# Two modulation chunks in another stage, and another order and other operands for two gates, in a two-layer decoder trunk

## The chip, the core and the metric

The kernel runs on one core of a Trainium2 chip. The core has five engines with instruction queues of their own: TensorE (PE, matrix products; its weight loads are listed as PEld), VectorE (DVE), ScalarE (ACT), GpSimd (POOL) and SyncE (SP, which here issues nearly all DMA transfers). They meet through semaphores. The metric is the device time of one execution in microseconds; lower is better. Times of repeated runs are compared by their median; one further execution is recorded by the hardware profiler.

## What is computed

The reference is a trunk of two layers on 256 tokens with 1,024 features, all in float32. A vector c sets shift, scale and gate (the modulation) of each of the four sub-layers. Cut to what matters here:

```python
for i in range(2):
    mod = silu(c) @ w_ada[i] + b_ada[i]          # 6 x 1024 values for each layer
    sh1, sc1, g1, sh2, sc2, g2 = split(mod, 6)
    h = rmsnorm(x) * (1 + sc1) + sh1
    y = dilated_mixture(h) if i == 0 else gla_mixer(h)
    x = x + g1 * y
    h = rmsnorm(x) * (1 + sc2) + sh2
    x = x + g2 * conv_ffn(h)
return rmsnorm(x)
```

The mixer of layer 0 is a mixture of three dilated window attentions with 16 heads. The mixer of layer 1 is a gated linear attention (GLA) with 4 heads in chunks of 64 tokens. For each chunk of a head it forms `A = causal(q_t @ k_t.T)`, `o = A @ v + q_t @ state`, and the mixer ends with `(rmsnorm(o) * silu(r)) @ w_out`, where r, the gate, is a product of h with 1,024 more columns. The channel mixer is `silu(a) * b` of two halves of a short convolution over `h @ w_up`, times w_down, with 2 x 2,816 columns.

## The kernel before

Features lie on the 128 partitions and the 256 tokens along the free dimension, so h is eight tiles of 128 x 256, one for each "k tile" of 128 features. To come near float32 with the fast float32r products each operand is split into a high and a low part, and each product is three matmuls (`mm3`, lines 199 to 201): high x high, low x high (the low part of h), and high x low (the low part of the weights). A weight tile is loaded by one DMA into a ring of four raw buffers (tile `raw`); ScalarE casts it into its high part (`whi`, line 172), and VectorE subtracts that from the raw data for the low part (`wlo`, line 178), each in two halves and into rings of three buffers (`split`).

The modulation is not a matrix product on TensorE. Its weights come in 48 chunks, 24 for each layer, each 1,024 KB, holding two columns of 128 outputs. A chunk is worked by `ada_dot` (line 140): for each half, VectorE multiplies 128 x 1,024 weights by silu(c), broadcast over the partitions, and sums them; then a small ScalarE operation (line 148 or 150) adds the bias. Eight chunks are worked at the start, where h is first built. The other 40 stand in the list `rest` and are taken in order, at places written out by hand: `next_half` takes half a chunk (512 KB) into one of three spare buffers of the attention stage, and `next_ada` takes a whole one into a buffer of the ring that the weights use.

The stages in order, on the profile's time axis: the start and the first products (to about 60 us); the attention by pairs of heads u = 0 to 7 (to about 287), where for u >= 2 each pair brings three query-key weight tiles (`wqk`, g = 0, 1, 2) and two value weight tiles (`wv`), and next_half is called behind each g; the output projection of layer 0; its up-projection (to about 419) in 22 column tiles of 48 matmuls each (`pab`), followed on VectorE by the convolution (lines 769, 771), the product (777) and the split of the result (779); its down-projection (`pd`, to about 479); the GLA (to about 573); its output projection (`py`, to 596); the up- and down-projection of layer 1; the final norm and output.

In the GLA, `states(hd)` forms a head's queries and keys (`pqk`), scales them on VectorE by the decays (k_d, q_t, k_t: lines 927 to 929), transposes k_d, and forms the products k_t x q_t (bank `a`, line 941), which VectorE copies through the causal mask into a_t (line 944). Then the states of the chunks follow (`kv`, line 951, and st, line 958). `products(hd)` forms the head's output from a_t, v, the states and q_t (bank `o`, lines 974 and 977), and `normed_output` norms it. `gate(n)` loads a weight tile of the gate (`w_r_b`) and forms its 48 matmuls into bank `pr`.

The order on each engine is fixed before the run. A scheduler goes through the program with a model of the engines' times: among the instructions that it holds ready on an engine it takes the first in program order, and it also places the buffers. `behind(i, ...)` makes instructions wait in that order until the named ones are issued. The program sets the gates between the heads' work as fillers for TensorE.

One more thing is set by hand: `shift(pool, columns)` places a pad, which moves the addresses of the tiles that the pool places behind it. A pad of 8 columns is 32 bytes on each partition. In the up-projections the column tiles i = 4 and 12 take, for the k tiles 6 and 7, copies of h (tile `lv`, made by ScalarE at line 740) that lie elsewhere in the memory. By the addresses that the kernel's tiles are given, the weights lie at 32 modulo 128 bytes, h at 96, and these copies at 32: level with the weights.

The few lines that the change touches most:

```python
def next_ada():
    if rest:
        ada_chunk(*rest.pop(0))
...
s2 = states(2)
output(1, *s1)
s3 = states(3)
po2 = products(2, *s2)
gate(0)
...
```

Of the kernel before, what the change touches and what calls it, by code (L numbers as in the profile page):

```python
# [57 lines left out]
def trunk(ctx: ExitStack, tc: tile.TileContext, I, out):  # L58
# [294 lines left out]
    def parts(w, at, n=P):  # L353
        return w[0][:, at : at + n], w[1][:, at : at + n]
# [225 lines left out]
    for u in range(NPAIR):  # L580
        with tc.issue_after(last_load[0].ins):
            bias = load_bias(u)
        q = [q_pair[u % 2]]
        k = [[att.tile([P, T + 4], F32R, tag=f"k0{i}", name="k") for i in range(2)]]
        for z in k[0]:
            nc.gpsimd.memset(z[:, T:].bitcast(F32), 0.0)
        for g in (1, 2):
            q.append(att.tile([P, T], F32, tag=f"q{g}", name="q"))
            k.append(att.tile([P, T], F32, tag=f"k{g}", name="k"))
        v = [att.tile([P, NG * P], F32, tag=f"v{t}", name="v") for t in range(2)]  # L590
        if u == 0:
            b0 = [bank("pqk", tg) for tg in "ssspp"]
            pqk = [b[:, T * i : T * i + T] for b in b0[:3] for i in range(2)]
            pv = b0[3:]
            b1 = [bank("pqk", "t") for _ in range(3)]
            pqk1 = [b[:, T * i : T * i + T] for b in b1 for i in range(2)]
            for kt in range(KT):
                s, e = kt == 0, kt == KT - 1

                for a, b in ((0, 0), (1, 0), (0, 1)):  # L600
                    for i in range(2 * NG):
                        w = parts(w0[kt], P * i)
                        mm(pqk[i], w[a], h[kt][b], start=s and i % 2 == 0 and (a, b) == (0, 0), stop=e and i % 2 == 1 and b == 1)  # L603
                wv = parts(w0[kt], 6 * P, NG * P)
                for a, b in ((0, 0), (1, 0), (0, 1)):
                    for t in range(2):
                        mm(pv[t][:, : NG * P], h[kt][a][:, P * t : P * t + P], wv[b], start=s and (a, b) == (0, 0), stop=e and b == 1)
                for i in range(2 * NG):
                    mm3(pqk1[i], parts(w0[kt], 9 * P + P * i), h[kt], s and i % 2 == 0, e and i % 2 == 1)
        if u < 2:  # L610
            for g in range(NG):
                evacuate(q, k, g, (pqk, pqk1)[u][2 * g], (pqk, pqk1)[u][2 * g + 1])
        else:
            for g in range(NG):
                w = split(I["wqk"][u - 2, g], 2048)
                pqk = bank("pqk", "p")
                pq, pk = pqk[:, :T], pqk[:, T:]
                for kt in range(KT):
                    s, e = kt == 0, kt == KT - 1
                    mm3(pq[:, :T], parts(w, 2 * P * kt), h[kt], s, False)  # L620
                    mm3(pk[:, :T], parts(w, 2 * P * kt + P), h[kt], False, e)
                done = evacuate(q, k, g, pq, pk)
                if (u, g) == (2, 0):
                    first_loads.append(last_load[0])
                    for _ in range(2):
                        next_half(outputs[0])

                for _ in range((3, 3 if u == 2 else 1, 2)[g]):
                    next_half(outputs[u - 1] if g == 1 else done)
            if u == 2:  # L630
                with behind(last_load[0]):
                    nc.sync.dma_start(x_all, I["xT"])
        if u > 0:
            pv = [bank("pv", "p") for _ in range(2)]
            for half in range(2):
                with behind(*chain[7]):

                    w = split(I["wv"][u - 1, half], 1536, after=((first_values,) if u == half == 1 else (), ()))
                for k4 in range(4):
                    kt = 4 * half + k4  # L640
                    wv = parts(w, 384 * k4, 384)
                    for t in range(2):
                        ht = [y[:, P * t : P * t + P] for y in h[kt]]
                        last_pv[:] = [mm3(pv[t][:, :384], ht, wv, kt == 0, kt == KT - 1)]
        for n in range(2):
            copies = by_group(v[n], pv[n], n)
            if u == n == 0:
                first_values = copies
        outputs.append(attend(u, q, k, v, bias))
# [67 lines left out]
    def ffn(l, early):  # L717
# [10 lines left out]
        with tc.tile_pool(name=f"ffn{l}", bufs=2) as pool:  # L728
# [6 lines left out]
            for i in range(NFF):  # L735
                if i == 2:
                    with behind(*chain[7]):
                        for kt in level:
                            for s in range(2):
                                nc.scalar.copy(level[kt][s], h[kt][s])  # L740
                if i == 0:

                    pab, pab1 = bank("pab", "t"), bank("pab")
                    for kt in range(KT):
                        mm3(pab[:, :T], parts(w_early[0], P * kt), h[kt], kt == 0, kt == KT - 1)
                        for s in range(2):
                            mm3(pab1[:, T * s : T * s + T], parts(w_early[1], 2 * P * kt + P * s), h[kt],
                                kt == 0 and s == 0, kt == KT - 1 and s == 1)
                    with behind(*chain[5]):
                        pu = [whole(pool.tile([P, T], F32, tag="u", name="u")), pab[:, :T]]  # L750
                elif i == 1:
                    pu = [pab1[:, :T], pab1[:, T:]]
                else:
                    with behind(*(chain[5], chain[7])[min(i - 2, 1)]):
                        w = split(I["w_up"][l, i], 2048)
                    pab = bank("pab")
                    pu = [pab[:, :T], pab[:, T:]]
                    for kt in range(KT):
                        hk = level.get(kt, h[kt]) if i in (4, 12) else h[kt]
                        for s in range(2):  # L760
                            mm3(pu[s], parts(w, 2 * P * kt + P * s), hk, kt == 0 and s == 0, kt == KT - 1 and s == 1)
                ab = []
                for s in range(2):
                    f = i + NFF * s
                    cw = [col(C_CW + 132 * l + 44 * j + f) for j in range(3)]
                    r = pool.tile([P, T], F32, tag=f"r{s}", name="r")
                    u = pu[s]
                    nc.scalar.activation(r, u[:, :T], AF.Identity, scale=cw[2], bias=col(C_CB + 44 * l + f))  # L768
                    nc.vector.scalar_tensor_tensor(r[:, 1:T], u[:, 0 : T - 1], cw[1], r[:, 1:T],
                                                   op0=ALU.mult, op1=ALU.add)  # L770
                    nc.vector.scalar_tensor_tensor(r[:, 2:T], u[:, 0 : T - 2], cw[0], r[:, 2:T],  # L771
                                                   op0=ALU.mult, op1=ALU.add)
                    ab.append(r)
                sa = pool.tile([P, T], F32, tag="sa", name="sa")
                silu = nc.scalar.activation(sa, ab[0], AF.Silu)
                g32 = pool.tile([P, T], F32, tag="g32", name="g32")
                nc.vector.tensor_tensor(g32, sa, ab[1], op=ALU.mult)
                nc.scalar.copy(g_hi[i], g32)
                last_g = nc.vector.tensor_tensor(g_lo[i], g32, g_hi[i].bitcast(F32), op=ALU.subtract)
                if l == 0 and i % 5 == 4 and i < 20:  # L780
                    with behind(*chain[7]):
                        next_ada()
            exp_ln_after(silu)
# [37 lines left out]
    nc.vector.tensor_scalar(nbg, small[:, C_BG : C_BG + 4], -1.0, None, op0=ALU.mult)  # L821

    PARTS = ((0, 1), (1, NH_B - 1))
    keep = gt([P, (NH_B - 1) * T], "keep", tag="D1")
    nc.gpsimd.memset(keep, 1.0)
    nc.gpsimd.memset(keep.rearrange("p (n c) -> p n c", c=CH)[:, :, 0:1], 0.0)
# [76 lines left out]
        nc.vector.tensor_copy(v[t][:, 512:D], pv[t][1])  # L903

    o_n = []
    turned_keys = []

    def states(hd):
        if hd == 0:
# [28 lines left out]
        pa = bank("a", "s")  # L938
        for t in range(2):
            c = slice(P * t, P * t + P)  # L940
            mm(pa[:, c], k_t[:, c], q_t[:, c], start=True, stop=True)
        a_t = gt([P, 2, P], "a_t", bufs=2)
        nc.gpsimd.memset(a_t, 0.0)
        nc.vector.copy_predicated(a_t, causal.bitcast(U32), pa[:, :T].rearrange("p (a b) -> p a b", a=2))
# [52 lines left out]
    def gate(n):  # L997

        w = split(I["w_r_b"][n], 2048, **({} if n else dict(after=(turned_keys[:1], ()), low=turned_keys[1:])))
        pr = bank("pr", "p")  # L1000
        for kt in range(KT):
            for s in range(2):
                with behind(*((), last_o, norm_ops[:1], ())[n]):
                    mm3(pr[:, T * s : T * s + T], parts(w, 2 * P * kt + P * s), h[kt],
                        kt == 0 and s == 0, kt == KT - 1 and s == 1)
        r = gt([P, (2, 3)[n % 2] * T], f"r{n}", tag=("r0", "C1", "r2", "cs1")[n])
        r_g.append(r[:, : 2 * T].rearrange("p (a b) -> p a b", a=2))
# [8 lines left out]
    s1 = states(1)  # L1016
    output(0, *s0)
    s2 = states(2)
    output(1, *s1)
    s3 = states(3)  # L1020
    po2 = products(2, *s2)
# [174 lines left out]
```

## Time and profile before

| | |
|---|---|
| median of 3 runs | 784.34 us (783.24, 784.34, 785.03) |
| the profiled execution, its own time | 787.82 us |
| its span, first to last instruction | 786.0 us |
| mean granted TensorE clock | 0.997 |
| read from memory | 182.59 MB |
| instructions | 15,983 |

How to read the rows below. A group's row has line, engine, operation, written tile <- read tiles, shapes and count, then busy time and the mean of one in ns. A row of the timeline begins with the start in us and the duration in us; what stands in square brackets is the engine's idle time just before it and what ended it. A row of the waits names who waited, for whom, how long in total, how often, and the longest. A row of a stretch has its start and end, its length, the busy time and the count of instructions of the engines asked for, the clock granted to TensorE as a share of full speed, the mean busy share of the DMA engines, and GB/s. Ends of matmuls are modelled, since they overlap: the time of one within a stream is the distance between starts.

### The profile page before, as it was taken

How to read it: one execution, taken by the hardware profiler on the slowest of the kernel's cores; microseconds unless marked ns; L12 is line 12 of the kernel's file. 1: busy time of each engine (PE TensorE's matmuls, PEld its weight loads, DVE VectorE, ACT ScalarE, POOL GpSimd, SP SyncE). 2: the span in 40 equal slices, each digit the busy share in tenths (PEclk: the TensorE clock that was granted, in tenths of full speed). 3: DMA queues.
4: the chain of work that ended last, by engine and by line, in shares of the span. 5: the costliest groups of instructions: out<-in, count | busy, mean ns of one | idle time of the engine just before them, and what ended most of it. 6: DMA issues, size and time to landing. Idle time of an engine off the chain costs nothing.

```text
span 786.0 us, 15983 instructions
## 1 busy us (share of the span) xinstructions
PE 772.8 (98%) x6430; PEld 746.8 (95%) x6430; DVE 644.8 (82%) x1160; ACT 483.0 (61%) x937; POOL 14.1 (2%) x40
## 2 busy tenths in 40 slices
PE   8999998999999999999999999999999999999997
PEld 5999987999999999999999998898999999999996
DVE  6987888889788868999998886797567898899662
ACT  5457555655556457867666656654667866667552
POOL 1000000000000010000000100000010000000000
PEclk9999999999999999999999999999999999999999
DMA  9989698777776527787645994966334765555741
GB/s 349 396 281 384 201 320 268 241 265 248 270 266 239 183 92 255 250 269 262 225 145 205 329 336 149 345 244 228 140 132 173 258 205 181 207 183 211 259 154 55
DMA packets 35497, 184.73 MB, mean 235 GB/s; under 512 B 6172, under 2 KB 7708, under 8 KB 21726
## 3 DMA queue, kind: packets, MB, share of 16 engines
q1 hardware_dynamic: 35040, 183.26, 66.4%
q8 instruction: 50, 0.82, 0.4%
q10 hardware_dynamic: 382, 0.45, 0.2%
q14 instruction: 25, 0.20, 0.1%
HBM read 182.59 MB, written 1.10 MB: 234 GB/s over the span
## 4 chain that ended last, share of the span: by engine, by line
PE 94%; DVE 3%; DMA 1%; issue 0%; ACT 0%; DVEq 0%
PE pab L201 10%; PE pab L200 10%; PE pab L199 10%; PE pqk L199 6%; PE pqk L200 5%; PE pqk L201 5%; PE pd L201 5%; PE pd L199 5%; PE pd L200 5%; PE pv L199 3%; PE pv L200 3%; PE pv L201 3%; PE pqk L603 2%; PE py L199 2%; PE py L200 2%; PE py L201 2%
## 5 line engine op out<-in xcount | busy, mean ns | idle before, releaser
L178 DVE TENSOR_TENSOR wlo<-raw,whi 128x1024 fp32r<-128x1024 f32 (+3 forms) x254 | 270.6, 1094 | 47.7 <-ACT whi L172 46.8
L172 ACT CAST whi<-raw 128x1024 fp32r<-128x1024 f32 (+4 forms) x270 | 243.2, 946 | 104.0 <-PE pab L200 40.7
L201 PE MATMUL pab<-hhi,wlo 128*128 128x256 f32 x672 | 184.7, 276 | 0.0
L200 PE MATMUL pab<-hlo,whi 128*128 128x256 f32 x672 | 184.6, 276 | 0.0
L199 PE MATMUL pab<-hhi,whi 128*128 128x256 f32 x672 | 183.2, 277 | 0.0
L200 PEld LDWEIGHTS pab<-hlo,whi 128*128 128x128 f32 x672 | 126.0, 188 | 0.2
L201 PEld LDWEIGHTS pab<-hhi,wlo 128*128 128x128 f32 x672 | 126.2, 188 | 0.0
L199 PEld LDWEIGHTS pab<-hhi,whi 128*128 128x128 f32 x672 | 125.1, 188 | 0.1
L140 DVE CUSTOM_DVE_ANT_0 ada_raw<-ada_raw,c_bc 128x1024 f32<-128x1024 f32 x96 | 113.3, 1218 | 10.2 <-DMA ada_raw<-in_w_ada 10.2
L199 PE MATMUL pqk<-hhi,whi 128*128 128x256 f32 x392 | 109.7, 285 | 1.3 <-DVE k L554 1.3
L200 PE MATMUL pqk<-hlo,whi 128*128 128x256 f32 x392 | 108.9, 283 | 0.0
L201 PE MATMUL pqk<-hhi,wlo 128*128 128x256 f32 x392 | 108.2, 283 | 0.0
L201 PE MATMUL pd<-ghi,wlo 128*128 128x256 f32 x352 | 97.1, 276 | 0.0
L200 PE MATMUL pd<-glo,whi 128*128 128x256 f32 x352 | 97.1, 276 | 0.0
L199 PE MATMUL pd<-ghi,whi 128*128 128x256 f32 x352 | 96.8, 276 | 0.0
L199 PEld LDWEIGHTS pqk<-hhi,whi 128*128 128x128 f32 x392 | 74.1, 190 | 2.1 <-DVE k L554 1.5
L201 PEld LDWEIGHTS pqk<-hhi,wlo 128*128 128x128 f32 x392 | 73.6, 191 | 0.8 <-issue 0.7
L200 PEld LDWEIGHTS pqk<-hlo,whi 128*128 128x128 f32 x392 | 74.1, 190 | 0.2
L200 PEld LDWEIGHTS pd<-glo,whi 128*128 128x128 f32 x352 | 66.1, 188 | 0.0
L201 PEld LDWEIGHTS pd<-ghi,wlo 128*128 128x128 f32 x352 | 66.1, 188 | 0.0
L199 PEld LDWEIGHTS pd<-ghi,whi 128*128 128x128 f32 x352 | 65.9, 188 | 0.0
L768 ACT ACTIVATE r<-pab,small 128x256 f32<-128x256 f32 x86 | 46.7, 559 | 15.5 <-DVE r L771 15.4
(224 smaller groups left out, 1370.6 us busy)
## 6 DMA issues: line engine op xcount, KB each, us to landing
raw<-in_w_up SPq DMA_DIRECT2D x42, 1024.0 KB, 4.9
ada_raw<-in_w_ada SPq DMA_DIRECT2D x27, 1024.0 KB, 6.0
raw<-in_w_down SPq DMA_DIRECT2D x32, 704.0 KB, 4.3
ada_raw<-in_w_ada SPq DMA_DIRECT2D x42, 512.0 KB, 6.0
raw<-in_wqk SPq DMA_DIRECT2D x18, 1024.0 KB, 5.7
raw<-in_wv SPq DMA_DIRECT2D x14, 768.0 KB, 6.1
raw<-in_w SPq DMA_DIRECT2D x7, 960.0 KB, 6.0
raw<-in_w_out_a SPq DMA_DIRECT2D x4, 1024.0 KB, 5.0
```

Source lines behind the costliest of these rows:

```text
L140: i = nc.vector.tensor_tensor_reduce(w, w, c_bc, op0=ALU.mult, op1=ALU.add, scale=1.0, scalar=0.0, accum_out=dot,)
L172: copied[0] = nc.scalar.copy(hi[:, c], raw[:, c])
L178: last_lo[0] = nc.vector.tensor_tensor(lo[:, c], raw[:, c], hi[:, c].bitcast(F32), op=ALU.subtract)
L199: mm(ps, a[0], b[0], start=start, stop=False)
L200: mm(ps, a[0], b[1], start=False, stop=False)
L201: return mm(ps, a[1], b[0], start=False, stop=stop)
L603: mm(pqk[i], w[a], h[kt][b], start=s and i % 2 == 0 and (a, b) == (0, 0), stop=e and i % 2 == 1 and b == 1)
L768: nc.scalar.activation(r, u[:, :T], AF.Identity, scale=cw[2], bias=col(C_CB + 44 * l + f))
```

## The change

It has three parts.

- Modulation. At u = 2 the two extra halves behind outputs[0] go, and behind g = 1 there is one half and not three; so u = 2 issues six halves, as the later pairs do. In layer 0's up-projection a whole chunk is taken behind each third column tile (i = 2, 5, 8, 11, 14, 17), not behind each fifth (4, 9, 14, 19). The list and its order are the same, so each place that follows takes the same chunk as before.
- First gate. The matmuls of gate(0) are issued behind the last matmul of line 941, which at that point is that of the last head (`last_a`).
- Second gate. A pad of 8 columns comes ahead of the GLA's tiles behind `nbg`. Behind states(2), ScalarE makes four copies of h (high and low part of the k tiles 6 and 7) in tiles that held the first head's decays (tags A0, B0, C0, D0), and gate(1) uses them in place of h for these two k tiles, in 12 of its 48 matmuls. By the addresses before, those four tiles lie at 0 modulo 128 bytes, and the pad takes them to 32.

```diff
@@ attention, pairs u >= 2
                 if (u, g) == (2, 0):
                     first_loads.append(last_load[0])
-                    for _ in range(2):
-                        next_half(outputs[0])
-
-                for _ in range((3, 3 if u == 2 else 1, 2)[g]):
+
+                for _ in range((3, 1, 2)[g]):
                     next_half(outputs[u - 1] if g == 1 else done)
@@ up-projection of layer 0
-                if l == 0 and i % 5 == 4 and i < 20:
+                if l == 0 and i % 3 == 2 and i < 20:
                     with behind(*chain[7]):
                         next_ada()
@@ GLA, its tiles
     PARTS = ((0, 1), (1, NH_B - 1))
+    shift(gla, 8)
     keep = gt([P, (NH_B - 1) * T], "keep", tag="D1")
@@ states(hd)
-            mm(pa[:, c], k_t[:, c], q_t[:, c], start=True, stop=True)
+            last_a[0] = mm(pa[:, c], k_t[:, c], q_t[:, c], start=True, stop=True)
@@ gate(n)
         for kt in range(KT):
+            hk = level.get(kt, h[kt]) if n == 1 else h[kt]
             for s in range(2):
-                with behind(*((), last_o, norm_ops[:1], ())[n]):
-                    mm3(pr[:, T * s : T * s + T], parts(w, 2 * P * kt + P * s), h[kt],
+                with behind(*(last_a, last_o, norm_ops[:1], ())[n]):
+                    mm3(pr[:, T * s : T * s + T], parts(w, 2 * P * kt + P * s), hk,
                         kt == 0 and s == 0, kt == KT - 1 and s == 1)
@@ order of the GLA, behind s2 = states(2)
+    level = {kt: [gt([P, T], "lv", F32R, tag=tg) for tg in tags] for kt, tags in ((6, ("A0", "B0")), (7, ("C0", "D0")))}
+    for kt in level:
+        for s in range(2):
+            nc.scalar.copy(level[kt][s], h[kt][s])
     output(1, *s1)
```

More of the change, by code (lines that the diff above doesn't have):

```diff
@@ L905, in trunk @@
     o_n = []
-    turned_keys = []
+    turned_keys, last_a = [], [None]
     def states(hd):
```

## The prediction

> **What bounds the kernel now.** I read the page's busy times and its chain first, then who makes TensorE wait.
>
> ```profile
> PE   772.8 (98%) x6430; PEld 746.8 (95%) x6430; DVE 644.8 (82%) x1160; ACT 483.0 (61%) x937; POOL 14.1 (2%) x40
> PE 94%; DVE 3%; DMA 1%; issue 0%; ACT 0%; DVEq 0%
> ```
> ```profile
> PE t L529 <- DVE pt L530: 1.4, 1, 1.4
> PE pqk L199 <- DVE k L554: 1.3, 1, 1.3
> PE pv L199 <- DVE k L554: 0.6, 1, 0.6
> PE o L974 <- DVE a_t L944: 0.6, 1, 0.6
> PE pr L201 <- DVE wlo L178: 0.5, 1, 0.5
> ```
>
> TensorE is busy 98% of the span and makes 94% of the chain that ended last, so a microsecond taken from another engine is worth nothing unless TensorE waits for it. Behind the start-up there is almost no such wait: the five above, all on VectorE. Three (3.3 us) lie in the attention around pair u = 2, two (1.1 us) in the last head of the gated attention (GLA). The change has one part for each place and a third for the pace of the matmuls themselves.
>
> **Part 1, the moved modulation chunks.** A half-chunk is one 512 KB load on SP's queue, one VectorE dot (line 140) and a tiny ScalarE operation. At u = 2 ten halves are issued; the change leaves six, the count of every later pair. The first stretch below is u = 2 and its surroundings, the second is pair 3, which has no loss (columns: stretch, its length, VectorE time in dots, count of instructions, granted clock, DMA share, GB/s).
>
> ```profile
> 95.00:135.00 40.00, 12.99 (x22) 0.96 0.86 291
> 135.00:166.00 31.00, 7.11 (x12) 1.00 0.71 238
> ```
> ```profile
> 92.08 1.21 DVE L140 CUSTOM_DVE_ANT_0 ada_raw<-ada_raw,c_bc 128x1024 f32<-128x1024 f32 x1
> 93.22 1.21 DVE L140 CUSTOM_DVE_ANT_0 ada_raw<-ada_raw,c_bc 128x1024 f32<-128x1024 f32 x1
> ...
> 105.14 1.21 DVE L140 CUSTOM_DVE_ANT_0 ada_raw<-ada_raw,c_bc 128x1024 f32<-128x1024 f32 x1
> 106.28 1.22 DVE L140 CUSTOM_DVE_ANT_0 ada_raw<-ada_raw,c_bc 128x1024 f32<-128x1024 f32 x1
> ...
> 113.45 1.23 DVE L140 CUSTOM_DVE_ANT_0 ada_raw<-ada_raw,c_bc 128x1024 f32<-128x1024 f32 x1 [1.64 <-DMA ada_raw<-in_w_ada]
> ```
>
> A dot costs 93.22 - 92.08 = 1.14 us of VectorE, so four fewer free 4.6 us there. Two are the pair at 92.08, ahead of the first wait at 104.9; two come out of the three from 105.14 on, ahead of the waits at 126 to 128. VectorE also stood 1.64 us at 113.45 for a chunk's load, and the change takes 4 x 512 KB off that stretch. 4.6 us of relief (6.2 with that load) against 3.3 us of waits: I take them as gone. They cost more than their length, as the granted clock shows (columns: stretch, length, TensorE busy, count, granted clock, DMA share, GB/s):
>
> ```profile
> 124.00:128.50 4.50, 1.63 (x11) 1.00 0.98 286
> 128.50:132.50 4.00, 4.00 (x22) 0.57 0.93 350
> ```
>
> TensorE ran 4.0 us at 0.57 of its clock, which loses 0.43 x 4.0 = 1.7 us. With the 3.3 us of waits the stall costs 5.0 us in this execution. [...]
>
> What it adds: two whole chunks (2 x 1,024 KB into the ring of four raw buffers, four dots) in layer 0's up-projection, and all six there now come every third column tile, not four every fifth. On SP's queue each load stands behind the w_up load of its own tile and ahead of the next one's. VectorE is the engine to fear (columns as in the first stretches, all VectorE work; the last two rows are the whole up-projection of layers 0 and 1):
>
> ```profile
> 318.00:356.00 38.00, 38.00 (x66) 1.00 0.77 265
> ...
> 301.00:420.00 119.00, 112.19 (x202) 1.00 0.68 236
> 600.00:718.00 118.00, 106.75 (x188) 1.00 0.59 202
> ```
>
> It has no free time from 318 to 356, and 119.0 - 112.2 = 6.8 us in the whole stage for 4.6 us more. What queues behind a dot is the low half of the next weights (wlo, line 178), and TensorE's third matmul of a tile waits for that. Tiles 3 and 4 are the tightest:
>
> ```profile
> 313.65 2.36 DVE L178 TENSOR_TENSOR wlo<-raw,whi 128x1024 fp32r<-128x1024 f32 x2 [1.10 <-ACT whi L172]
> ...
> 317.73 1.23 DVE L178 TENSOR_TENSOR wlo<-raw,whi 128x1024 fp32r<-128x1024 f32 x1 [1.32 <-ACT whi L172]
> ```
> ```profile
> 315.76 0.28 PE L201 MATMUL pab<-hhi,wlo 128*128 128x256 f32 x1
> ...
> 321.20 0.28 PE L201 MATMUL pab<-hhi,wlo 128*128 128x256 f32 x1
> ```
>
> Tile 3's first half is ready about 314.8 and wanted at 315.76, a lead of 0.9 us; tile 4's about 318.9 against 321.20, 2.2 us. A chunk is 2.3 us. The chunk of tile 2 can take the place that tile 4's has now, ahead of tile 3's low part; the next one's load comes after two or three more weight loads and meets tile 4 or later, where 2.2 us nearly covers it. Price: 0 to 1.4 us (2.3 - 0.9); I take 0, covered by that lead.
>
> **Part 2, the first gate behind the last head's masked products** (pa, line 941).
>
> ```profile
> 543.17 0.28 PE L200 MATMUL pr<-hlo,whi 128*128 128x256 f32 x1
> 543.94 0.38 PE L201 MATMUL pr<-hhi,wlo 128*128 128x256 f32 x1 [0.49 <-DVE wlo L178]
> ...
> 549.89 0.61 PE L941 MATMUL a<-q_t,k_t 128*128 128x128 f32 x4
> 551.11 0.49 PE L974 MATMUL o<-a_t,v 128*128 128x128 f32 x2 [0.61 <-DVE a_t L944]
> ```
> ```profile
> 542.34 0.41 DVE L929 TENSOR_TENSOR k_t<-pqk,e_k 128x256 f32<-128x256 f32 x1
> ```
>
> Now the gate's 48 matmuls go first, stopping at 543.94 for their low weights, and pa comes at 549.89; its mask on VectorE then keeps TensorE until 551.11. From 549.89 to 551.11 is 1.2 us. Put first, pa needs k_t, done at 542.75, so it starts where the gate starts now and lies in the gap before 543.94; the mask then lies behind the gate's matmuls. Nothing is added. Gain 1.2 us; bounds: 0 if VectorE masks only behind the gate weights already in its queue and TensorE meets it anyway, 1.7 if the 0.5 us wait goes too.
>
> **Part 3, copies level with the weights.** One form of matmul, 128x256, has two paces. Fast in the feed-forward layers, slow in the gates and the output projection of layer 1:
>
> ```profile
> 350.18 0.28 PE L201 MATMUL pab<-hhi,wlo 128*128 128x256 f32 x1
> ...
> 351.20 0.28 PE L201 MATMUL pab<-hhi,wlo 128*128 128x256 f32 x1
> ```
> ```profile
> 575.06 0.28 PE L201 MATMUL py<-ohi,wlo 128*128 128x256 f32 x1
> ...
> 576.12 0.28 PE L201 MATMUL py<-ohi,wlo 128*128 128x256 f32 x1
> ```
>
> Nine matmuls lie between the rows of each pair: 1.02 / 9 = 113 ns and 1.06 / 9 = 118 ns. Around a norm's two matmuls at 556.9 the second gate itself changes pace, three matmuls in 0.36 us before and in 0.34 us behind:
>
> ```profile
> 556.26 0.28 PE L201 MATMUL pr<-hhi,wlo 128*128 128x256 f32 x1
> 556.62 0.28 PE L201 MATMUL pr<-hhi,wlo 128*128 128x256 f32 x1
> ...
> 558.10 0.28 PE L201 MATMUL pr<-hhi,wlo 128*128 128x256 f32 x1
> 558.44 0.28 PE L201 MATMUL pr<-hhi,wlo 128*128 128x256 f32 x1
> ```
>
> So the pace is a state that a break can turn over and that then holds. The feed-forward layers already use copies of h (lv) for k tiles 6 and 7 of tiles 4 and 12, and are fast behind them. The change gives gate 1 the same copies, after which gates 2 and 3 (96 matmuls) and the projection (192) run without a break: 288 x 4.4 ns = 1.3 us if the copies turn the pace, less their own cost:
>
> ```profile
> L199 PE MATMUL pab<-lv,whi 128*128 128x256 f32 x16 | 4.5, 281 | 0.0
> L199 PE MATMUL pab<-hhi,whi 128*128 128x256 f32 x672 | 183.2, 277 | 0.0
> ...
> 309.04 0.74 ACT L740 CAST lv<-hlo 128x256 fp32r<-128x256 f32 x2
> ```
>
> A matmul on a copy takes some 5 ns longer, 0.1 us for 12. The four copies cost ScalarE 4 x 0.37 = 1.5 us, covered by its idle time (page: 61% busy); without that cover a head's transposed keys come up to 1.5 us late, and TensorE has other matmuls to run. No run shows the copies turning a slow pace fast, so the bounds are -0.1 and +1.3; I take 1.2, nearer the feed-forward rows. The 32-byte pad ahead of the GLA tiles moves their addresses; I price it within those bounds.
>
> **The sum.** The profiled execution took 787.82 us (span 786.0 and 1.8 around it): 5.0 + 1.2 + 1.2 - 0 = 7.4 off, 780.4. It lies 3.5 us above the median of the runs, 784.34. TensorE is paced evenly nearly everywhere, so that excess can lie only in the start-up and in the stalls. The slow clock (1.7 us) is about the spread of the three runs (783.24 to 785.03), so I count it as not in every run, and the u = 2 stall as 3.3: 3.3 + 1.2 + 1.2 = 5.7, and 784.34 - 5.7 = 778.6 us, with 776.9 where the clock's part is there too.
>
> **Rivals.**
>
> The pace doesn't turn: gates and projection stay at 118 ns. For it: the copies of the feed-forward layers stand in a stream that was fast before them. 784.34 - 3.3 - 1.2 + 0.1 = 779.9 us. [...]
>
> The stall moves: VectorE is as full behind u = 2 as in it, the bias rows and weight loads keep DMA at 0.86, and another VectorE result comes late in place of lines 530 and 554. Or the profiled execution's excess of 3.5 us lies in this stall and plain runs have only 5.0 - 3.5 = 1.5 of it. Either way about half of the 3.3 is left to gain: 784.34 - 1.6 - 1.2 = 781.5 us. Against it: pair 3, with the count that u = 2 gets, has no wait.
>
> Slower: the moved dots make layer 0's up-projection wait, and the break turns its pace. Place: the low weights of tile 3 or 4. Price: a chunk ahead of tile 3's half is 2.3 - 0.9 = 1.4 us; from tile 4 on 18 x 48 + 528 = 1,392 matmuls at 4.4 ns more are 6.1 us. It decides once a dot pair stands ahead of a low half whose lead is under 2.3 us and the copies at tile 12 don't bring the pace back; then part 3 earns nothing either: 784.34 - 3.3 - 1.2 + 1.4 + 6.1 = 787.3 us. For it: the gate's change of pace above, and no free VectorE time from 318 to 356. Against it: from tile 5 on the weights run ahead, and layer 1 shows the stage's pace holding.
>
> No change: the four dots cost as much in layer 0 as they cost at u = 2, without the change of pace: up to 4.6 us of waits against 3.3 + 1.2. 784.4 us.
>
> **How the numbers follow.** Forecast (stall gone, gate gained, pace turned) 0.42; pace stays 0.20; stall moves 0.18; slower 0.12; no change 0.08. The likeliest gives 778.6, its own range being 776.9 to 780. The whole range reaches down to 776.0 (776.9, and 0.9 if some 200 of the gates' and heads' products ahead of the copies, at 4.4 ns each, turn fast through the pad as well) and up past the rival at 781.5 to 783.0, leaving out no change and slower, 0.20 together. A measurement of this kernel tells about 0.2% (1.6 us) from no change: under 782.8 is faster (0.42 + 0.20 + 0.18 = 0.80), over 785.9 slower (0.12), between them 0.08.
>
> **What would show it.** Right: in the list of TensorE's waits the rows of lines 530 and 554 are gone and the granted clock stays 1.00 from 124 to 135; pa comes ahead of the first gate's matmuls and no wait on a_t is left; the projection's rows stand 113 ns apart; layer 0's up-projection keeps 5.4 us a tile (48 x 113 ns). Wrong: a TensorE wait on line 178 near tiles 3 to 6, feed-forward rows 118 ns apart, or a projection still at 118. A third of the gain missing with all of these right would mean that plain runs never had the stall that the profile shows.

## The result, and the profile after

The changed kernel takes 786.67 us (median of 9 runs, 785.99 to 791.25), the kernel before 782.46 us beside it (median of 9, 779.41 to 785.03). The ratio is 1.0057 with a 95% interval of 1.0037 to 1.0077: slower by some 4.5 us (4.2 by the medians), where 5.7 us less were forecast. The profiled execution took 786.39 us, of which its span is 784.6.

First the same views as before. The page's busy times and the engines' shares of the chain that ended last:

```profile
PE 767.2 (98%) x6430; PEld 742.8 (95%) x6430; DVE 643.4 (82%) x1160; ACT 485.5 (62%) x941; POOL 13.9 (2%) x40
...
PE 90%; DVE 5%; ACT 2%; DMA 1%; issue 1%; ACTq 0%; DVEq 0%
```

TensorE is as full as it was, but its share of the chain fell from 94% to 90% and VectorE's rose from 3% to 5%: somewhere TensorE now waits on VectorE. The list of TensorE's waits says where:

```profile
PE ms L211 <- DVE oacc L985: 5.9, 1, 5.9
PE cb L123 <- DMA c_row<-in_c: 3.1, 1, 3.1
PE pqk L199 <- DVE k L554: 1.0, 1, 1.0
PE t L529 <- DVE pt L530: 0.7, 1, 0.7
PE pv L199 <- DVE k L554: 0.6, 1, 0.6
```

Two things are to be read here. The waits around u = 2 shrank from 3.3 to 1.0 + 0.7 + 0.6 = 2.3 us but did not go. And one new wait of 5.9 us stands first; the matmuls `ms` of line 211 form the mean square in a head's norm. The timeline around it, some rows of TensorE, VectorE and ScalarE in the changed kernel:

```profile
536.06 0.41 DVE L928 TENSOR_TENSOR k_t<-pqk,e_k 128x256 f32<-128x256 f32 x1
...
536.39 5.75 DVE L178 TENSOR_TENSOR wlo<-raw,whi 128x1024 fp32r<-128x1024 f32 x5
538.52 0.59 ACT L983 ACTIVATE osq<-o 128x512 f32<-128x512 f32 x1
...
542.07 0.41 DVE L985 TENSOR_TENSOR oacc<-osq 128x256 f32<-128x256 f32 x1
...
542.63 1.19 PE L211 MATMUL ms<-oacc,ones_d 128*128 128x256 f32 x2 [5.89 <-DVE oacc L985]
...
543.61 1.06 PE L940 MATMUL a<-q_t,k_t 128*128 128x128 f32 x4
...
544.33 0.56 PE L199 MATMUL pr<-hhi,whi 128*128 128x256 f32 x1
```

The last head's k_t was ready at 536.5, so pa could have started. But in TensorE's fixed order the norm of head 1 stands ahead of pa: `output(1)` precedes `states(3)` in the program. That norm needs `oacc`, the sum of head 1's squares, and on VectorE `oacc` stands behind five low halves of the gates' weights, 5.75 us of work. ScalarE made the squares (osq) at 539.1, behind five casts of the same weights, so VectorE's queue is what came last.

The kernel before had the same queue and the same order. Its rows for these instructions:

```profile
542.67 5.76 DVE L178 TENSOR_TENSOR wlo<-raw,whi 128x1024 fp32r<-128x1024 f32 x5
542.95 0.39 PE L199 MATMUL pr<-hhi,whi 128*128 128x256 f32 x1
...
548.34 0.42 DVE L986 TENSOR_TENSOR oacc<-osq 128x256 f32<-128x256 f32 x1
...
549.46 0.59 PE L211 MATMUL ms<-oacc,ones_d 128*128 128x256 f32 x2
```

There the late sum cost nothing, because TensorE meanwhile ran the first gate's 48 matmuls, which were free to go first. The change tied exactly those matmuls to pa, behind the norm. The granted clock added to the price (columns: stretch, length, TensorE busy, count, granted clock, DMA share, GB/s; the changed kernel):

```profile
539.80:546.65 6.85, 4.02 (x17) 0.50 1.00 416
546.65:560.00 13.35, 13.35 (x116) 1.00 0.17 56
```

TensorE was granted half speed for 6.85 us, 4.0 of them with matmuls, which loses an estimated 0.5 x 4.02 = 2.0 us. So part 2 costs 5.9 + 2.0, and gives 1.2 (the mask, as forecast) and 0.5 (the gate's wait for its low weights): 6.2 us. From the norm ahead of the GLA (first matmul `early`) to the first matmul of its output projection (`py`) the profile of before took 94.5 us and this one 100.4, with some of part 3's gain in it.

The drop begins inside the gap of 5.9 us: TensorE fell idle at 542.63 - 5.89 = 536.74, and the clock fell at 539.8, 3.1 us later. It was back at 546.65. The drop at u = 2 in the profile of before was also at 0.50 and half as long, from 128.88 to 132.28. What sets the moment and the length of a drop is not shown.

### The profile page after: what moved, and what is told of

Its sections match the earlier page's. It is cut to its first block, busy times and chain, and to the rows that moved or that the text cites. A ratio compares the mean times of both kernels' runs of the same rounds, so it can differ in the third digit from the quotient of the medians.

```text
span 784.6 us, 15965 instructions
## 1 busy us (share of the span) xinstructions
PE 767.2 (98%) x6430; PEld 742.8 (95%) x6430; DVE 643.4 (82%) x1160; ACT 485.5 (62%) x941; POOL 13.9 (2%) x40
## 4 chain that ended last, share of the span: by engine, by line
PE 90%; DVE 5%; ACT 2%; DMA 1%; issue 1%; ACTq 0%; DVEq 0%
PE pab L201 10%; PE pab L200 10%; PE pab L199 10%; PE pqk L199 5%; PE pd L201 5%; PE pd L199 5%; PE pd L200 5%; PE pqk L200 5%; PE pqk L201 5%; PE pv L199 3%; PE pv L200 3%; PE pv L201 3%; PE py L199 2%; PE py L201 2%; PE py L200 2%; DVE ada_raw L140 2%
```

## The experiments

Each is given as an edit of the changed kernel or of the one before. The first four take the change apart. They ran on one chip, beside a kernel before of 783.97 us (median of 29 runs, 780.45 to 787.28).

**Without part 2.**

```diff
-                with behind(*(last_a, last_o, norm_ops[:1], ())[n]):
+                with behind(*((), last_o, norm_ops[:1], ())[n]):
```

> The changed kernel without part 2 (the first gate is free again to run ahead of the last head's masked products); parts 1 and 3 stay. Theory A: the whole loss of the change is part 2. In TensorE's order the masked products stand behind the norm of head 1, whose sum (oacc) stands on VectorE behind five low halves of gate weights (5.75 us); without the gate's 48 matmuls ahead of that norm TensorE stands 5.9 us and then runs 4.0 us of matmuls at half clock (2.0 us lost). Then here no TensorE wait on oacc is left, the granted clock stays 1.00 until the end, and the time is 2.5 to 5 us under before (part 1: 2.0 to 4.0, part 3: 0.9), 777.5 to 780 if before is at 782.5. Rival B: the moved chunks or the copies cost the time in plain runs, where the profile doesn't show it: then it stays over before, 784 or more.

Measured: 781.13 us (12 runs, 778.83 to 783.71), ratio 0.9968 (0.9952 to 0.9984). The same part of the GLA takes 94.1 us against 100.4, and the difference, 6.2 us before rounding, is the 6.2 worked out above. The wait on oacc is gone; the first gate waits again for its low weights and the last head for its mask, as in the kernel before:

```profile
537.68 0.38 PE L201 MATMUL pr<-hhi,wlo 128*128 128x256 f32 x1 [0.49 <-DVE wlo L178]
...
543.02 0.59 PE L211 MATMUL ms<-oacc,ones_d 128*128 128x256 f32 x2
...
543.46 0.61 PE L940 MATMUL a<-q_t,k_t 128*128 128x128 f32 x4
...
544.67 0.49 PE L973 MATMUL o<-a_t,v 128*128 128x128 f32 x2 [0.60 <-DVE a_t L943]
```

**Part 2 alone**, in the kernel before.

```diff
-            mm(pa[:, c], k_t[:, c], q_t[:, c], start=True, stop=True)
+            last_a[0] = mm(pa[:, c], k_t[:, c], q_t[:, c], start=True, stop=True)
...
-                with behind(*((), last_o, norm_ops[:1], ())[n]):
+                with behind(*(last_a, last_o, norm_ops[:1], ())[n]):
```

> The kernel before with part 2 alone. Theory A: the same wait of 5 to 6 us of TensorE on oacc and a half clock behind it: 5.9 + 2.0, less the 1.2 to 1.6 us that the old waits in this place cost, so about 6.5 us over before (789 at 782.5). Rival B: within 1.5 us of before.

Measured: 790.66 us (6 runs, 788.44 to 792.3), ratio 1.0090 (1.0064 to 1.0116), that is 6.7 us more. Its wait stands at the same place with the same length, and the clock falls during it (rows of its waits, and of a stretch as above):

```profile
PE ms L211 <- DVE oacc L986: 5.9, 1, 5.9
```
```profile
543.30:550.10 6.80, 5.12 (x22) 0.50 0.87 358
```

**Part 1 alone**, in the kernel before.

```diff
-                    for _ in range(2):
-                        next_half(outputs[0])
-                for _ in range((3, 3 if u == 2 else 1, 2)[g]):
+                for _ in range((3, 1, 2)[g]):
...
-                if l == 0 and i % 5 == 4 and i < 20:
+                if l == 0 and i % 3 == 2 and i < 20:
```

> The kernel before with part 1 alone (two chunks moved to layer 0's up-projection). If the stall at pair u = 2 stands in plain runs as it does in the profile of before: 3.5 to 5.0 us under before. If only the profiled execution had most of it: 0 to 2 us under. If the chunks cost layer 0's up-projection a wait or its pace: at or over before, with a TensorE wait on the low weights between 295 and 420 us. The changed kernel's profile had 117.5 us for the 1,032 matmuls there, as before, so I expect no cost and 2.5 us under.

Measured: 782.28 us (12 runs, 779.31 to 785.17), ratio 0.9982 (0.9963 to 1.0000): 1.7 us less, and anything from 0 to 2.9 is inside the interval. The 2.5 us expected are not excluded, nor is the case of 0 to 2 us, in which the profiled execution alone had most of the stall; 3.5 us and more are.

**Part 3 alone**, pad and copies, in the kernel before.

```diff
+    shift(gla, 8)
...
+            hk = level.get(kt, h[kt]) if n == 1 else h[kt]
...
+    level = {kt: [gt([P, T], "lv", F32R, tag=tg) for tg in tags] for kt, tags in ((6, ("A0", "B0")), (7, ("C0", "D0")))}
+    for kt in level:
+        for s in range(2):
+            nc.scalar.copy(level[kt][s], h[kt][s])
```

> The kernel before with part 3 alone (pad, copies of h in the second gate). If the copies turn the pace: the output projection's 192 matmuls in 21.8 us and not 22.6, the gates behind them at 113 ns a matmul, and 1.2 us under before. If the pace in the changed kernel was turned by its other order of matmuls in the gated attention (part 2), not by the copies: the projection stays at 22.6 us and the time at before's, within 0.3 us.

Measured: 783.53 us (12 runs, 781.32 to 784.96), ratio 0.9996 (0.9979 to 1.0014): not to be told from no change. The case expected for a turned pace came only in part: in its profile the projection took 21.76 us, not 22.6, but the 1.2 us are missing from the time.

So -1.7, +6.7 and -0.4 make +4.6, about the 4.5 of the whole change: part 2 is the whole loss. The next two runs ask what in part 2 makes it, both beside a kernel before of 783.29 us (22 runs).

**Head 1's norm moved behind pa**, with part 2 as it is. TensorE's order becomes pa, first gate, norm of head 1.

```diff
-    output(1, *s1)
+    po1 = products(1, *s1)
     s3 = states(3)
+    normed_output(1, po1, last_a)
     po2 = products(2, *s2)
```

> The changed kernel with one thing moved: head 1's products are formed as before, but its norm is issued behind the last head's masked products, so that in TensorE's order pa comes first, then the first gate's matmuls, and head 1's norm behind them. Theory (the loss of the change is that the first gate, which filled the 5.9 us in which head 1's sum of squares is late, went behind that norm): the wait of 5.9 us on oacc goes, the clock stays full through the gated attention, and the wait on a_t goes too (1.2 us under the kernel without part 2); 780 us beside a kernel before of 784, and early-query to projection 93 to 94 us against 100.4 in the changed kernel. Rival A (the gate's low weights, which still come behind k_t on VectorE, are the wait): the gate stands for 0.5 to 3 us on wlo and the kernel ties with the one without part 2, 781 us. Rival B (any place behind pa is too late, since the last head's keys are late themselves): a wait of 3 us or more on k_t or wlo, 784 us or more.

Measured: 780.17 us (11 runs, 779.25 to 783.08), ratio 0.9963 (0.9947 to 0.9979). Its timeline is what part 2 was taken for in the prediction:

```profile
539.23 3.49 DVE L178 TENSOR_TENSOR wlo<-raw,whi 128x1024 fp32r<-128x1024 f32 x3
...
539.50 0.71 PE L940 MATMUL a<-q_t,k_t 128*128 128x128 f32 x4
...
539.97 0.36 PE L199 MATMUL pr<-hhi,whi 128*128 128x256 f32 x1
...
542.63 0.44 DVE L943 COPY_PREDICATED a_t<-causal,a 128x256 f32<-128x256 uint32 x1
...
545.23 0.42 DVE L985 TENSOR_TENSOR oacc<-osq 128x256 f32<-128x256 f32 x1
...
545.84 0.59 PE L211 MATMUL ms<-oacc,ones_d 128*128 128x256 f32 x2
```

The same five low halves are ahead of oacc (three, the mask, two more), and again the sum comes late; but TensorE has the gate to run until 545.8, and neither `ms` nor a_t's reader waits.

**The sum moved ahead of the weights** instead, with part 2's order kept: the casts of gates 0 and 1 behind the square, their low halves behind the sum.

```diff
-        nc.scalar.activation(sq, po, AF.Square)
+        squared_out = nc.scalar.activation(sq, po, AF.Square)
...
-        nc.vector.tensor_tensor(acc, sq[:, 0:T], sq[:, T : 2 * T], op=ALU.add)
+        summed[:] = squared_out, nc.vector.tensor_tensor(acc, sq[:, 0:T], sq[:, T : 2 * T], op=ALU.add)
...
-        w = split(..., **({} if n else dict(after=(turned_keys[:1], ()), low=turned_keys[1:])))
+        w = split(..., **(dict(after=(summed[:1], summed[:1]), low=summed[1:], late=summed[1:]) if n < 2 else {}))
```

> The changed kernel, with its order on TensorE kept (norm of head 1, then pa, then the first gate), but the casts and low halves of the weights of gates 0 and 1 are issued behind head 1's square (ScalarE) and its sum (VectorE). Theory (the five low halves of 1.15 us each ahead of oacc on VectorE, and the five casts ahead of osq on ScalarE, are what the norm waits for): the wait of 5.9 us on oacc falls to under 1.5 us; but the gate's weights are now made later, so the gate itself waits on wlo or whi for 1 to 4 us. 782 to 785 us. Rival (the sum is late because head 1's output itself is late, not because of the queue ahead): the wait on oacc stays at 4 us or more, and the time at 786 or more.

Measured: 781.67 us (12 runs, 780.41 to 782.93), ratio 0.9981 (0.9968 to 0.9994). The waits of TensorE in the GLA:

```profile
PE pr L199 <- ACT whi L172: 1.1, 1, 1.1
PE pr L201 <- DVE wlo L178: 1.0, 2, 0.8
...
PE ms L211 <- DVE oacc L985: 0.2, 1, 0.2
```

The wait on the sum falls from 5.9 to 0.2 us with TensorE's order unchanged, which shows the gates' weights queued ahead of it as the cause. The edit moves ScalarE's casts as well as VectorE's low halves, so it does not part the two. 2.1 us come back as waits of the gates for their weights, in the range expected, though the total is a little under it.

**Is part 2 worth anything once mended?** The kernel without part 2 and the one with head 1's norm moved, both again, on one chip (kernel before 783.73 us, 15 runs).

> The kernel without part 2 (parts 1 and 3) a second time, beside the next one on the same chip. Its last head keeps TensorE for 1.2 us on the mask, so it should be the slower of the two by 0.9 to 1.2 us. 781 us.

> The changed kernel with head 1's norm issued behind the last head's masked products, a second time, on the same chip as its sibling without part 2. Theory (part 2 was worth its 1.2 us once the norm is out of the way): 0.9 to 1.2 us under the sibling, 780 us. Rival (the 1.2 us are given back by the second gate or the last norm, as only the whole time can tell): a tie within 0.4 us.

Measured: 780.33 us (10 runs, 778.7 to 781.41), ratio 0.9957 (0.9940 to 0.9975), and 779.72 us (6 runs, 777.67 to 780.08), ratio 0.9941 (0.9919 to 0.9963). By the medians the mended one is 0.6 us ahead; the intervals overlap. In the profiles the GLA (counted as above) takes 94.1 and 94.3 us without part 2, and 93.3 and 93.4 with it mended: 0.9 us less in both pairs. That is a little under the forecast's 1.2, and the mended version has the lowest median of the kernels that were run repeatedly. That the mended part 2 makes the whole kernel faster than leaving it out is therefore not shown.

**What turns the pace?** Three single executions of the kernel without part 2: copies without the pad, the pad without copies, a pad of 16 without copies. The first drops `shift(gla, 8)`, the second has `level = {}`, the third has both `level = {}` and `shift(gla, 16)`.

> The kernel without part 2 (parts 1 and 3), with the pad of 8 columns left out: the copies of h are made and used, but stand at 0 modulo 128 bytes, not level with the weights at 32. Theory (copies level with the weights turn the slow pace, 118 ns a matmul, into the fast one, 113): the second gate from its k tile 6 on, the third, the fourth and the projection stay at 118 ns, projection 22.6 us, time 1.3 us over its sibling. Rival (any copy elsewhere, or the break alone, turns the pace): projection 21.8 us.

> The kernel without part 2 (parts 1 and 3), with the pad kept and the copies left out: gate 1 uses h for all k tiles. Theory (the copies turn the pace): gates 2 and 3 and the projection stay at 118 ns, projection 22.6 us. Rival (the pad, by the addresses of the projection's own operands, is what made it fast): projection 21.8 us, gates 2 and 3 at 5.65 us each.

> The kernel without part 2, no copies of h, and a pad of 16 columns (64 bytes) in place of 8. Theory (the second gate, the later ones and the projection run slow only if their operands lie at certain addresses, and the pad of 8 took them off these): a pad of 16 may lie either way, but then gates 2 and 3 and the projection hold one pace throughout, 113 or 118 ns. Rival (the pace is set anew at each break, whatever the addresses): the paces before and behind the norm in the second gate differ, as they did in the kernel before.

All three ran the projection fast, 21.76 us (779.3, 779.75 and 778.78 us). The theory of the first two (only copies level with the weights turn the pace) did not hold: copies at 0 modulo 128 bytes were followed by a fast projection, and so was each pad without copies. The third does not decide: from the third gate on it held one pace, as its theory has it, but its second gate went from 113 to 118 and back to 113 ns a matmul at its breaks, which was the sign of its rival. The fourth is the kernel with part 1 alone, which has neither pad nor copies, profiled a second time.

> The kernel before with part 1 alone (no pad, no copies), a second look. Its projection took 22.6 us in the first one. Theory (the pace follows from the kernel's addresses and its order): 22.6 us again, with the second gate fast between its two breaks and the rest slow, matmul for matmul as before. Rival (the pace is a matter of chance in each execution): 21.8 us, or other stretches slow.

Its projection was fast this time (781.36 us). One row of the tile `py` from each of its two profiles (shortest, median and longest duration in ns, first and last start in us), in order:

```profile
L201 PE MATMUL py<-ohi,wlo x64: 281/281/281, 567.3 to 589.5; 128*128 128x256 f32 x64
```
```profile
L201 PE MATMUL py<-ohi,wlo x64: 276/276/276, 568.0 to 589.4; 128*128 128x256 f32 x64
```

The first stretches over 22.2 us, the second over 21.4, for the same program, so the same addresses. The theory of that run (the pace follows from addresses and order) is wrong: the same program ran at both paces. The two executions were on different chips, so whether the execution or the chip decides is open.

## Why the prediction was wrong, step by step

**Part 2 is the step that failed**: "Put first, pa needs k_t, done at 542.75, so it starts where the gate starts now and lies in the gap before 543.94; the mask then lies behind the gate's matmuls. Nothing is added." The text asked when pa's operands were ready and not what stands ahead of pa on TensorE. The row for `ms` at 549.46, just ahead of pa at 549.89, was in the trace of before. The edit did not pull pa forward; it pushed the gate back behind pa and with it behind head 1's norm. Its size is then plain from the profile of before: without the gate TensorE has nothing from 542.95 on, the sum is there at 548.34 + 0.42 = 548.76, and the difference of 5.8 us is the wait. Neither bound (0 and 1.7 us) reached below nothing, and the rival on the slower side sat in another stage. What was right is that the mask can be hidden: with the norm out of the way 0.9 us were gained in the GLA.

Most of the signs named for a right prediction came true: pa ahead of the first gate, no wait on a_t, a projection at 113 ns, a granted clock of 1.00 from 124 to 135; the rows of lines 530 and 554 stayed. The time rose all the same, because no sign asked for waits that the new order itself would make.

**Part 1** was right in kind and too large in size. The u = 2 waits shrank by 1.0 us of 3.3, not wholly. The term that was too large is "4.6 us of relief (6.2 with that load) against 3.3 us of waits: I take them as gone". Relief earlier in VectorE's queue is not relief just ahead of the late result. Before line 554's copy stand two low halves, in the kernel before (126.06 to 127.80) as in the changed one:

```profile
119.93 1.82 DVE L178 TENSOR_TENSOR wlo<-raw,whi 128x768 fp32r<-128x768 f32 x2
121.66 0.42 DVE L554 COPY k<-pqk 128x256 f32<-128x256 f32 x1
...
122.14 0.39 PE L199 MATMUL pqk<-hhi,whi 128*128 128x256 f32 x1 [0.98 <-DVE k L554]
```

In every profile the waits of `t` and `pqk` are 1.4 and 1.3 us with the old count and 0.7 and 1.0 with the new. The third, of `pv`, is in one of the three profiles with the old count (0.6 us) and in five of the eleven with the new (0.6 to 1.6), so the count does not remove it.

The slow clock was said to be "not in every run". All three profiles with the old count show it there (before, part 2 alone, part 3 alone: as little as 0.77, 0.81 and 0.63 granted over 5 us), and three of the eleven with the new count (0.74, 0.74 and 0.69). From the first matmul of `pqk` to the first of `pab`, the attention and its projection took 284.3, 282.8 and 284.1 us with the old count and 279.4 to 282.2 (mean 281.1) with the new one: 2.7 us, or 2.4 when the first 40 matmuls of `pqk`, slow in the profile of before, are left out; against 1.7 in the plain runs and 3.3 in the sum.

Its costing at nothing in layer 0's up-projection held. The two more chunks are there (first row the changed kernel, VectorE in dots; second and third its whole stage, VectorE and TensorE), and TensorE has no idle time:

```profile
297.50:416.50 119.00, 14.16 (x12) 1.00 0.70 246
```
```profile
297.50:416.50 119.00, 113.79 (x202) 1.00 0.70 246
```
```profile
297.50:416.50 119.00, 119.00 (x1051) 1.00 0.70 246
```

So the rival on the slower side, with its time near the measured one (787.3 us), had the wrong mechanism: no dot made TensorE wait in that stage, and the pace stayed fast (119.00 us for 1,051 matmuls, 113 ns each). That its time came near is chance.

The rival of the moved stall has a slip in its sum: 784.34 - 1.6 - 1.2 takes off only one of the two gains of 1.2 us that it leaves standing. With both it is 780.3, not 781.5.

**Part 3**: the projection ran at 21.76 / 192 = 113 ns a matmul as forecast. The two rows of `py`, before and changed:

```profile
L201 PE MATMUL py<-ohi,wlo x64: 281/281/281, 573.6 to 595.9; 128*128 128x256 f32 x64
```
```profile
L201 PE MATMUL py<-ohi,wlo x64: 276/276/276, 573.0 to 594.4; 128*128 128x256 f32 x64
```

But the forecast treated the slow pace of the profile as a property of the kernel before. The profiles without copies were fast in four of six, so plain runs of the kernel before may well have the gain already in a part of them. The median moved by less than the 1.2 us taken: 0.4, within its interval of nothing. One program, that with part 1 alone, ran at both paces, over 22.2 and 21.4 us in the rows of `py` shown with it, so the addresses alone do not set the pace; where the two paces come from is not shown.

**The base.** The profiled execution's excess of 3.5 us over the median was laid to the start-up and the stalls together. By the profiles it was mostly the start-up. TensorE in the stretch from 12 to 20 us, before and changed:

```profile
12.00:20.00 8.00, 8.00 (x32) 1.00 1.01 417
```
```profile
12.00:20.00 8.00, 8.00 (x64) 1.00 1.02 422
```

TensorE is busy throughout in both, with half as many matmuls in the first. The same twelve `warm` matmuls, before and changed, show that it ran there at about half speed:

```profile
14.72 2.93 PE L297 MATMUL warm<-ones_d 128*128 128x128 f32 x12
```
```profile
12.92 1.60 PE L297 MATMUL warm<-ones_d 128*128 128x128 f32 x12
```

The column's 1.00 misleads here: the trace's first record of a granted clock, at full speed, begins only at 19.65 us before and at 10.76 in the changed kernel. The first of `pqk` came at 17.3 us there, at 14.3 here, and between 13.1 and 16.6 in the other profiles. The profile at 16.6 (head 1's norm moved) also lies above the median of its runs, by 2.9 us.

## What to carry to other kernels

Before tying work behind an instruction, read what stands ahead of that instruction on its own engine, not only when its operands are ready; a filler that covers a late result must not be queued behind the reader of that result. A wait that costs nothing in the profile may be covered by just the work that one is about to move: look up each result that falls due in the stretch, and ask what the engine would run in its place. And where one profile shows a state (a pace, a clock), look at a second execution before pricing a change of it. Relief of a queue counts only where it stands ahead of the late result.

## What was not expected of the hardware

**Two paces of one matmul form**, 113 and 118 ns, hold over long stretches, and the same program takes the one or the other in two executions. Three programs were profiled twice and all three show it: part 1 alone in layer 1's output projection (281 and 276 ns in the rows of `py`), head 1's norm moved at the end of layer 0's (276 and 281), and the kernel without part 2 behind layer 1's, where the two executions took 192.1 and 190.2 us to the end (the first alone has a wait of 0.8 us for low weights). Each time it was on two different chips, so the chip is not excluded as the reason. What turned a slow stretch fast without a break were matmuls on copies. Layer 1's up-projection in the kernel with part 2 alone, its third products before and behind the copies of tile 4:

```profile
L201 PE MATMUL pab<-hhi,wlo x66: 281/281/281, 603.0 to 626.0; 128*128 128x256 f32 x66
...
L201 PE MATMUL pab<-hhi,wlo x122: 276/276/279, 627.8 to 668.9; 128*128 128x256 f32 x122
```

Of the 28 up-projections in the fourteen profiles, six begin slow. All six hold 118 ns for some 204 matmuls and run at 113 from the copies of tile 4 on, and the 22 others keep 113 before and behind those copies: so in this stage the copies do turn the pace, which the prediction had found in no run. For gate 1 this is not shown. All eight profiles with copies there have a fast projection, and four of the six without; but where the gate was slow ahead of its copies (part 3 alone, and copies without the pad), a break stands just ahead of them (part 3 alone: a matmul of 471 ns at 556.2, the copies from 556.5). Why a stretch starts slow is open.

**The clock's drop at u = 2** follows gaps of 1.4 and 1.3 us with work between them in all three profiles with the old count. With the new one the gaps are 0.7 and 1.0 us in all eleven, and the clock dropped in three of them. A later gap of 1.6 us in the second profile with head 1's norm moved brought no drop. So the length of a single gap does not decide it here.
